# Seven instead of four SwiGLU pairs made of seven products, and where their weights' sums are made

## The chip, the cores and the metric

The kernel runs on one core of a Trainium2 chip. The time is that of one execution on the device, in microseconds, the median of several runs. The core has five engines that run beside each other and wait for one another by semaphores: PE (TensorE, matmuls into PSUM), DVE (VectorE) and ACT (ScalarE) for element-wise work, POOL (GpSimd), and SP (SyncE), which here issues all transfers between HBM and the core's SBUF from one queue, in a fixed order.

## The reference

A decoder block on 512 positions of 1024 channels, all in float32. Two token mixers run beside each other, are merged by gates, and are followed by a SwiGLU channel mixer with 2816 hidden channels:

```python
h = rmsnorm(x, norm1_g[l])
z = h @ w_in[l] + b_in[l]
z_glu, z_rx, z_rg, z_ga, z_gb = jnp.split(z, split_idx, axis=-1)
...                                   # y_a: convolution branch, y_b: recurrence branch
m = jax.nn.sigmoid(z_ga) * y_a + jax.nn.sigmoid(z_gb) * y_b
x = x + m @ w_mix_out[l]
h = rmsnorm(x, norm2_g[l])
x = x + (jax.nn.silu(h @ ffn_w1[l]) * (h @ ffn_w3[l])) @ ffn_w2[l]
```

and a last rmsnorm. The change concerns the last line quoted: the two products with ffn_w1 and ffn_w3, and the preparation of their weights and of those of ffn_w2.

## The kernel before, in words

**Numbers in two parts.** PE multiplies float32 values in a reduced form (F32R). Each operand is split into an upper part (a cast on ACT, L117) and a lower part (a subtraction on DVE or POOL, L113), and each product is made of three matmuls: upper by upper, upper by lower, lower by upper. Weights come in chunks of 128 x 1024 through four raw buffers (pool `raws`, RAW = 4) and are split into five `hl` buffers (HL = 5). `weights(key)` (L161) takes a chunk for use and first has the loads and splits of the next four chunks (AHEAD = 4) written into the program. Tiles named raw_x and hl_x in the profile belong to the chunk family x: in (w_in), lo and co (the mixers' output weights), mxb and mxt (w_mix_out), f (ffn_w1 and ffn_w3, plain), fb and ft (the same for seven products), ob and ot (ffn_w2).

**Stages.** The input stage multiplies by w_in (PE tiles z, g) in an order written out by hand (`ORDER`), with the convolution and the layer norm running beside it on DVE and ACT in small steps. The input stage's chunks have their lower parts made on POOL, all later ones on DVE. After it come the products of the recurrence branch (yb, 8 steps), of the convolution branch (ya, 8 steps), the mixing product (mxr), the SwiGLU stage (f, fr) and the output product (or).

**The SwiGLU stage.** The 22 tiles of 128 hidden channels go in 11 pairs (k, k + 11). A plain pair takes four chunks and 96 matmuls with 512 columns. Pairs in `SEVEN`, which are 2 to 5, use seven products of half-size blocks instead of eight (a Strassen-Winograd form, `ffn_seven`, L1011): seven chunks, called b11, b21, b22, t2, t1, t3, t4 in the order of use, and 168 matmuls with 256 columns, 24 a product. The b chunks are blocks of ffn_w1 and ffn_w3 side by side; the t chunks are sums of blocks.

**The weights' sums.** The t chunks are made earlier and kept in HBM. `make_f_sums` (L315) does so in the input stage, a piece at a time: from step 4 on, every third step of `ORDER`, it loads a piece (four quarters of 128 x 256, two transfers, tile fws, three buffers), makes four POOL operations from it two steps later, and stores it to `fs` (512 KB) five chunks later. There are four pieces a pair, 16 in all; whatever is left is done after the yb steps. The output weights ffn_w2 need the same kind of sums (`Quartered.make_sums`, L276): two raw buffers are loaded, DVE does four operations of 128 x 512 (tile ows), and four stores of 256 KB (ot) follow. These eleven are the last weights' sums. `out_sums(n)` (L959) writes n of them into the program: two after pair 1, one after each of pairs 3 and 5, two after each later pair until all are done.

**A pair's own work.** When both tiles of a pair exist, `Sevenfold.pair` (L825) makes from them what the output product needs: a split of 128 x 512 (ous), a sum and a split of 128 x 256 (os, os1p) and three subtractions of 128 x 256 (oe, ov). It stands at the end of the pair. The tiles live in a pool of 63 slots.

**Order.** Engines work through fixed queues. Outside the stretches written by hand, a planner that goes by estimated durations sets the order when the kernel is made; of what is ready it takes what comes earlier in the program. A buffer that comes free goes to the next tile in its pool. `issue_after` ties instructions behind a given one on its engine.

Of the kernel before, what the change touches and what calls it, by code (L numbers as in the profile page):

```python
# [8 lines left out]
F32 = mybir.dt.float32  # L9
F32R = mybir.dt.float32r  # L10
# [3 lines left out]
P = 128  # L14
T = 512
# [25 lines left out]

SEVEN = (2, 3, 4, 5)
SUMS_AT, SUMS_STEP, SUMS_LAG, STORE_LAG = 4, 3, 2, 5


ROWS = [
# [32 lines left out]
def tile_block(ctx, tc, a, out):  # L81
    nc = tc.nc
# [1 line left out]
    consts = pool("consts", 1)  # L84
    raws = pool("raws", RAW)
    hls = pool("hls", HL)
    wsums = pool("wsums", 3)
    psum = pool("psum", 6, space=bass.MemoryType.PSUM)
    psum2 = pool("psum2", 2, space=bass.MemoryType.PSUM)

# [131 lines left out]

    dram = ctx.enter_context(tc.tile_pool(name="dram", bufs=1, space=bass.MemoryType.DRAM))

    class Quartered:
        def __init__(self, name, w, kh, lo, parts=()):

            self.name, self.w, self.kh = name, w, kh
            self.parts = {n: [None] * kh for n in parts}
            self.sums = {(n, k): dram.tile([P, T], F32, tag=f"{name}{n}_{k}", name=f"{name}{n}_{k}") for n in ("t1", "t2", "t3", "t4") if n not in parts for k in range(kh)}  # L230
            self.at = {}

            def quarter(n, k):
                if n[0] == "t":
                    return self.sums[n, k][:, :]
# [40 lines left out]
        def make_sums(self, k):  # L276
            q = [raws.tile([P, 1024], F32, tag="raw", name=f"{self.name}ws{k}_{i}") for i in range(2)]
            for i, v in enumerate(q):
                nc.sync.dma_start(v, self.w[:, k + self.kh * i, :])
            (q11, q12), (q21, q22) = ((v[:, :T], v[:, T:]) for v in q)  # L280
            sub(vec, q22, q22, q12)
            sub(vec, q12, q12, q11)
            vec.tensor_tensor(out=q11, in0=q22, in1=q11, op=ALU.add)
            sub(vec, q21, q21, q11)
            for n, v in (("t1", q12), ("t2", q11), ("t3", q22), ("t4", q21)):
                if n in self.parts:
                    self.parts[n][k] = split(f"{self.name}{n}{k}", v, vec)
                else:
                    nc.sync.dma_start(self.sums[n, k][:, :], v)
# [4 lines left out]


    KF = NF // 2
    F_SUMS = ("t2", "t1", "t4", "t3")
# [7 lines left out]
    def f_chunk(n, k):  # L305
        def load(raw_t):
            if n[0] == "t":
                nc.sync.dma_start(raw_t, f_sums[k][:, F_SUMS.index(n), :])
            else:
                for i, w_ in enumerate((w1, w3)):  # L310
                    nc.sync.dma_start(raw_t[:, i * T : (i + 1) * T].rearrange("p (k n) -> p k n", k=4), f_quarter(n, k, w_, 0, 4))

        wchunk(f"f{n}_{k}", load, 8, P, lo=vec)

    def make_f_sums():  # L315

        todo = [(k, i, c) for k in SEVEN for i in range(2) for c in (0, 2)]
        sums_due, stores_due = [], []  # L320
        n = 0
        while todo or sums_due or stores_due:
            if stores_due and emitted[0] >= stores_due[0][0]:
                stores_due.pop(0)[1]()
            if sums_due and n >= sums_due[0][0]:
                sums_due.pop(0)[1]()
            if todo and n >= SUMS_AT and (n - SUMS_AT) % SUMS_STEP == 0:
                k, i, c = todo.pop(0)
                raw = wsums.tile([P, 1024], F32, tag="wsum", name=f"fws{k}_{i}_{c}")
                q = [raw[:, 256 * m : 256 * m + 256] for m in range(4)]  # L330
                four = (w1, w3)[i].rearrange("p (h k) (e n) -> p h k e n", h=2, e=2)
                with tc.issue_after(newest["load"]):
                    for h in range(2):
                        nc.sync.dma_start(
                            raw[:, h * T : h * T + T].rearrange("p (e k n) -> p e k n", e=2, k=2),
                            four[:, h, c : c + 2, :, k * P : (k + 1) * P].rearrange("p k e n -> p e k n"),
                        )

                def sums(raw=raw, q=q, k=k, at=T * i + P * c):
                    q11, q12, q21, q22 = q  # L340
                    with tc.issue_after(newest["sub"]):
                        sub(pool_e, q22, q22, q12)
                        sub(pool_e, q12, q12, q11)
                        pool_e.tensor_tensor(out=q11, in0=q22, in1=q11, op=ALU.add)
                        sub(pool_e, q21, q21, q11)

                    def stores():
                        with tc.issue_after(newest["load"]):
                            nc.sync.dma_start(f_sums[k][:, :, at : at + 256], raw.rearrange("p (m n) -> p m n", m=4))
# [443 lines left out]
            mixq.make_sums(j // 2 - 1)  # L793
    yb = sgb
    run_beside(1000)
    for _ in f_sums_steps:
        pass


    add = lambda o, x, y: vec.tensor_tensor(out=o, in0=x, in1=y, op=ALU.add)  # L800
# [8 lines left out]

    class Sevenfold:  # L810
        def __init__(self, q):
            self.q, self.uv, self.ops = q, [], []
            self.name, self.kh = q.name, q.kh

        def tile(self, j, make):

            k, i = j % self.kh, j // self.kh
            if i == 0:
                self.uv.append((longt(f"{self.name}u{k}"), longt(f"{self.name}v{k}")))
            for dst, cs in zip(self.uv[k], HALVES):  # L820
                make(cs, dst[:, HALVES[i]])
            if i:
                self.pair(k, *self.uv[k])

        def pair(self, k, ua, va):  # L825

            n = self.name
            u_ = split(f"{n}us{k}", ua, vec)
            s1 = shortt(f"{n}s1{k}")[:, LO]
            add(s1, va[:, LO], va[:, HI])  # L830
            sp = longt(f"{n}s1p{k}", F32R)
            split_to(sp[:, LO], sp[:, HI], s1, vec)
            e = longt(f"{n}e{k}")
            sub(vec, e[:, HI], ua[:, LO], va[:, LO])
            sub(vec, va[:, LO], s1, ua[:, LO])
            sub(vec, e[:, LO], ua[:, HI], va[:, LO])
            self.ops.append((u_, sp, e, va))
# [116 lines left out]


    o7 = Sevenfold(outq)
    sums_of = iter(range(KF))

    def out_sums(n):  # L959

# [50 lines left out]
    def ffn_seven(k):  # L1011
# [151 lines left out]
```

## Time and profile before

| | us |
|---|---|
| median of three runs | 814.86 (813.67 to 815.19) |
| the profiled execution | 814.89 |
| its span | 813.0 |
| PE busy | 800.0 |
| DVE busy | 644.1 |
| ACT busy | 443.1 |
| POOL busy | 210.3 |
| input stage, to the last z matmul | 325 |
| plain pairs 0 and 1 | 463 to 511 |
| pairs 2 to 5, seven products | 511 to 592 |
| plain pairs 6 to 10 | 592 to 700 |
| output product and end | 700 to 813 |

The span runs from the first to the last instruction that the profiler saw; the execution's own time is 1.9 us longer. In the profile's rows an instruction is named by engine, line, operation and out<-in; a line is often that of a helper (L113 the subtraction, L117 the cast, L441 three matmuls per product), so that tiles tell more than lines. In the timelines a row has its start, its length, the number of merged instructions, and in brackets how long the engine was idle before it and what ended that. The table of stretches gives for each stretch the busy time of every engine with the number of instructions, PE's granted clock as a share of full speed, the busy share of the DMA engines and their GB/s. Matmuls overlap, so that a matmul's listed duration is longer than its distance from the next.

### The profile page before, as it was taken

Reading aid. Unit: us, or ns where it says so; the run is one execution under the profiler, and the core shown is the slowest. Engines: PE = TensorE matmul, PEld = TensorE weight load, DVE = VectorE, ACT = ScalarE, POOL = GpSimd, SP = SyncE. Lnnn points to the kernel's source line nnn. Section 1 sums busy time; section 2 is a strip of 40 time slices with the busy share of each in tenths; the row PEclk is TensorE's granted clock in tenths of the full one; section 3 lists DMA queues with packets and bytes.
Section 4 is the critical chain, followed back from the end, with each engine's and each line's share of the span. In section 5 each row is a group of like instructions: output and inputs, shape, how many; then the busy total and the mean of one; then the engine's idle time right before and its main releaser. Section 6 shows DMA issues by size and latency. Waiting matters only on the chain.

```text
span 813.0 us, 11453 instructions
## 1 busy us (share of the span) xinstructions
PE 800.0 (98%) x4038; PEld 683.3 (84%) x4038; DVE 644.1 (79%) x1010; ACT 443.1 (55%) x626; POOL 210.3 (26%) x156
## 2 busy tenths in 40 slices
PE   8999999999999999999999999999999999999996
PEld 7988888888887888888888898999988888888884
DVE  4699899998999987777878769797875664688456
ACT  7546688776687755653336554364632223476442
POOL 3565768766675740000000042000000000000000
PEclk9999999999999999999999999999999999999998
DMA  6646475666654522358638535788778778576542
GB/s 209 193 123 171 136 202 176 189 193 198 186 170 130 182 75 65 116 171 263 217 104 259 156 97 176 238 262 248 224 247 282 249 271 297 177 250 216 169 160 104
DMA packets 182029, 153.46 MB, mean 189 GB/s; under 512 B 12519, under 2 KB 150163, under 8 KB 181971
## 3 DMA queue, kind: packets, MB, share of 16 engines
q1 hardware_dynamic: 181971, 152.72, 60.7%
q8 instruction: 32, 0.52, 0.3%
q14 instruction: 26, 0.21, 0.1%
HBM read 123.46 MB, written 26.21 MB: 184 GB/s over the span
## 4 chain that ended last, share of the span: by engine, by line
PE 93%; DVE 4%; issue 1%; DMA 1%; SPq 0%; POOL 0%; ACT 0%; POOLq 0%
PE z L441 31%; PE f L441 19%; PE or L844 13%; PE fr L1020 10%; PE yb L441 7%; PE ya L441 5%; PE mxr L844 5%; DVE cv L600 2%; PE g L721 2%; DMA raw_in<-in_w_in_dram 1%; PE th L481 0%; DVE xb L745 0%; PE tx L481 0%; DVE of L1086 0%; SPq L397 0%
## 5 line engine op out<-in xcount | busy, mean ns | idle before, releaser
L600 DVE SCALAR_TENSOR_TENSOR cv<-u,par,cv 128x511 f32<-128x511 f32 (+17 forms) x240 | 162.6, 729 | 1.1 <-ACT cv L597 0.9
L113 POOL TENSOR_TENSOR hl_in<-raw_in,hl_in 128x1024 fp32r<-128x1024 f32 x52 | 125.5, 2418 | 94.0 <-ACT hl_in L117 92.0
L117 ACT CAST hl_in<-raw_in 128x1024 fp32r<-128x1024 f32 x52 | 54.3, 1044 | 5.9 <-PE z L441 3.0
L117 ACT CAST hl_f<-raw_f 128x1024 fp32r<-128x1024 f32 x28 | 29.3, 1050 | 49.1 <-DMA raw_f<-in_ffn_w_dram 36.0
L113 DVE TENSOR_TENSOR hl_ob<-raw_ob,hl_ob 128x1024 fp32r<-128x1024 f32 (+1 forms) x23 | 27.1, 1178 | 26.8 <-ACT hl_ob L117 26.6
L113 DVE TENSOR_TENSOR hl_f<-raw_f,hl_f 128x1024 fp32r<-128x1024 f32 x28 | 36.2, 1304 | 14.3 <-ACT hl_f L117 14.2
L994 POOL TENSOR_TENSOR hf<-h20h,h20l 128x512 f32<-128x512 f32 x1 | 1.3, 1287 | 171.8 <-DVE h20l L485 171.8
L117 ACT CAST hl_ob<-raw_ob 128x1024 fp32r<-128x1024 f32 (+1 forms) x23 | 23.4, 1015 | 40.3 <-PE or L844 17.4
L441 PE MATMUL z<-h10h,hl_in 128*128 128x512 f32 (+1 forms) x112 | 42.4, 380 | 2.7 <-DVE h10l L485 1.5
L441 PE MATMUL z<-h15h,hl_in 128*128 128x512 f32 (+1 forms) x112 | 42.0, 376 | 0.0
L441 PE MATMUL z<-h16h,hl_in 128*128 128x512 f32 (+1 forms) x112 | 42.0, 376 | 0.0
L441 PE MATMUL z<-h17h,hl_in 128*128 128x512 f32 (+1 forms) x112 | 41.9, 376 | 0.0
L441 PE MATMUL z<-h11h,hl_in 128*128 128x512 f32 (+1 forms) x112 | 41.8, 375 | 0.0
L441 PE MATMUL z<-h12h,hl_in 128*128 128x512 f32 (+1 forms) x112 | 41.8, 375 | 0.0
L441 PE MATMUL z<-h14h,hl_in 128*128 128x512 f32 (+1 forms) x112 | 41.8, 375 | 0.0
L441 PE MATMUL z<-h13h,hl_in 128*128 128x512 f32 (+1 forms) x112 | 41.8, 375 | 0.0
L113 POOL TENSOR_TENSOR fws<-fws 128x256 f32<-128x256 f32 x48 | 36.3, 756 | 2.3
L113 DVE TENSOR_TENSOR ows<-ows,ows 128x512 f32<-128x512 f32 x22 | 15.2, 689 | 20.6 <-DMA ows<-in_ffn_w_dram 20.4
L113 DVE TENSOR_TENSOR hl_ot<-raw_ot,hl_ot 128x1024 fp32r<-128x1024 f32 (+1 forms) x17 | 20.1, 1191 | 11.1 <-ACT hl_ot L117 10.7
L441 PEld LDWEIGHTS z<-h10h,hl_in 128*128 128x128 f32 x112 | 21.3, 191 | 7.4 <-DVE h10l L485 1.8
L117 ACT CAST hl_ot<-raw_ot 128x1024 fp32r<-128x1024 f32 (+1 forms) x17 | 17.5, 1028 | 16.5 <-PE or L844 14.8
L441 PEld LDWEIGHTS z<-h15h,hl_in 128*128 128x128 f32 x112 | 21.4, 191 | 3.8
(905 smaller groups left out, 2574.9 us busy)
## 6 DMA issues: line engine op xcount, KB each, us to landing
raw_in<-in_w_in_dram SPq DMA_DIRECT2D x52, 512.0 KB
raw_f<-in_ffn_w_dram SPq DMA_DIRECT2D x28, 512.0 KB
ows<-in_ffn_w_dram SPq DMA_DIRECT2D x22, 512.0 KB
ot<-ows SPq DMA_DIRECT2D x44, 256.0 KB
raw_ob<-in_ffn_w_dram SPq DMA_DIRECT2D x33, 256.0 KB
raw_ot<-ot SPq DMA_DIRECT2D x33, 256.0 KB
fws<-in_ffn_w_dram SPq DMA_DIRECT2D x32, 256.0 KB
fs<-fws SPq DMA_DIRECT2D x16, 512.0 KB
```

The source lines that it names most:

```text
L113: return eng.tensor_tensor(out=o, in0=x, in1=y, op=ALU.subtract)
L117: copy(h, full)
L441: pe.matmul(ps, l, r, start=i == 0, stop=i == n - 1)
L600: vec.scalar_tensor_tensor(out=acc[c][:, s:], in0=u[c][:, : T - s], scalar=dw(c, s), in1=acc[c][:, s:], op0=ALU.mult, op1=ALU.add)
L721: pe.matmul(ps, l, r, start=k == 0, stop=k == len(mms) - 1)
L844: pe.matmul(banks[i], l_[:, ts], r_, start=start and n == 0, stop=stop and n == 2, skip_group_check=again)
L994: pool_e.tensor_tensor(out=v, in0=h2p[c][0].bitcast(F32), in1=h2p[c][1].bitcast(F32), op=ALU.add)
L1020: pe.matmul(ps[:, HALVES[i]], lw[:, 4 * i + c, :], rx_, start=not (again or i or c or m), stop=bool(i and c == 3 and m == 2), skip_group_c ...
```

## The change

- `SEVEN` grows to pairs 2 to 8. Three plain pairs become pairs of seven products.
- The input stage makes 28 pieces instead of 16. Steps 4 to 49 take every third step as before; from step 49 on (`SUMS_DENSE`) a piece starts at every second step, up to step 73. The generator goes on through the ya steps and is emptied after them. It could also make last weights' sums early (`OUT_EARLY`), which is set to none.
- The last weights' sums are placed by `OUT_SUMS`: four after pair 1, one after each of pairs 2 to 8, none later. The four results of one lie side by side in one HBM tile, and are stored in two transfers of 512 KB instead of four of 256 KB.
- A pair's own work is put in a waiting list. A pair of seven products no longer does it at its end: it is released in the middle of the next one, behind its second output block. Pairs 6, 7 and 8 keep it waiting (`keep = k - 6`), and plain pair 9 releases all three at its start. The tiles ous of pairs 0 to 2 go to the three buffers of the pieces, which have no other use by then.

```diff
-SEVEN = (2, 3, 4, 5)
+PIECES = 3
+OUT_EARLY = 0
+OUT_SUMS = {1: 4, 2: 1, 3: 1, 4: 1, 5: 1, 6: 1, 7: 1, 8: 1}
+SEVEN = (2, 3, 4, 5, 6, 7, 8)
 SUMS_AT, SUMS_STEP, SUMS_LAG, STORE_LAG = 4, 3, 2, 5
+SUMS_DENSE = 49
...
+            self.all_sums = [dram.tile([P, 4, T], F32, tag=f"{name}t_{k}", name=f"{name}t_{k}") for k in range(kh)]
...
+            if not self.parts:
+                for i, v in enumerate(q):
+                    nc.sync.dma_start(self.all_sums[k][:, 2 * i : 2 * i + 2, :], v.rearrange("p (m n) -> p m n", m=2))
+                return
...
-            if stores_due and emitted[0] >= stores_due[0][0]:
+            if stores_due and (emitted[0] >= stores_due[0][0] or not (todo or sums_due)):
...
-            if todo and n >= SUMS_AT and (n - SUMS_AT) % SUMS_STEP == 0:
-                k, i, c = todo.pop(0)
+            if todo and n >= next_at:
+                next_at += SUMS_STEP - (n >= SUMS_DENSE)
+                name, halves, dest = todo.pop(0)
...
-    for _ in f_sums_steps:
-        pass
...
-                self.pair(k, *self.uv[k])
+                self.waiting.append((k, *self.uv[k]))
+                self.release()
+
+        def release(self, keep=0):
+            while len(self.waiting) > keep:
+                self.pair(*self.waiting.pop(0))
...
-            u_ = split(f"{n}us{k}", ua, vec)
+            p_ = None
+            if n == "o" and k < PIECES:
+                both = wsums.tile([P, 1024], F32R, tag="wsum", name=f"{n}us{k}")
+                p_ = both[:, :T], both[:, T:]
+            u_ = split(f"{n}us{k}", ua, vec, p_)
...
         if n == 0:
             mixq.make_sums(3)
+        next(f_sums_steps, None)
+    for _ in f_sums_steps:
+        pass
...
         out_of(c12, u_[:, HI])
+        o7.release(max(0, k - 6))
         product(r7, "s3", "t3")
...
-        o7.pair(k, u_, v_)
+        o7.waiting.append((k, u_, v_))

     for k in range(1, KF):
         if k in SEVEN:
             ffn_seven(k)
-            out_sums(k % 2)
+            out_sums(OUT_SUMS.get(k, 0))
             continue
+        o7.release()
...
-        out_sums(2 if k < KF - 1 else KF)
+        out_sums(OUT_SUMS.get(k, 0))
```

More of the change, by code (lines that the diff above doesn't have):

```diff
@@ L86, in tile_block @@
     hls = pool("hls", HL)
-    wsums = pool("wsums", 3)
+    wsums = pool("wsums", PIECES)
     psum = pool("psum", 6, space=bass.MemoryType.PSUM)
@@ L223, in tile_block @@
     dram = ctx.enter_context(tc.tile_pool(name="dram", bufs=1, space=bass.MemoryType.DRAM))
+    IN_PLACE = ("t2", "t1", "t4", "t3")
     class Quartered:
@@ L229, in __init__ @@
             self.parts = {n: [None] * kh for n in parts}
-            self.sums = {(n, k): dram.tile([P, T], F32, tag=f"{name}{n}_{k}", name=f"{name}{n}_{k}") for n in ("t1", "t2", "t3", "t4") if n not in parts for k in range(kh)}
+            self.all_sums = [dram.tile([P, 4, T], F32, tag=f"{name}t_{k}", name=f"{name}t_{k}") for k in range(kh)]
+            self.sums = {(n, k): self.all_sums[k][:, i, :] for i, n in enumerate(IN_PLACE) if n not in parts for k in range(kh)}
             self.at = {}
@@ L234, in quarter @@
                 if n[0] == "t":
-                    return self.sums[n, k][:, :]
+                    return self.sums[n, k]
                 i, h = int(n[1]) - 1, int(n[2]) - 1
@@ L288, in make_sums @@
                 else:
-                    nc.sync.dma_start(self.sums[n, k][:, :], v)
+                    nc.sync.dma_start(self.sums[n, k], v)
     mixq = Quartered("mx", a["w_mix_out"][0].rearrange("(k p) n -> p k n", p=P), ND // 2, vec, ("t1", "t4"))
@@ L296, in tile_block @@
     KF = NF // 2
-    F_SUMS = ("t2", "t1", "t4", "t3")
     f_sums = {k: dram.tile([P, 4, 1024], F32, tag=f"fs{k}", name=f"fs{k}") for k in SEVEN}
@@ L307, in load @@
             if n[0] == "t":
-                nc.sync.dma_start(raw_t, f_sums[k][:, F_SUMS.index(n), :])
+                nc.sync.dma_start(raw_t, f_sums[k][:, IN_PLACE.index(n), :])
             else:
@@ L315, in make_f_sums, with f_piece, o_piece @@
     def make_f_sums():
-        todo = [(k, i, c) for k in SEVEN for i in range(2) for c in (0, 2)]
+        def f_piece(k, i, c):
+            four = (w1, w3)[i].rearrange("p (h k) (e n) -> p h k e n", h=2, e=2)
+            at = T * i + P * c
+            halves = [four[:, h, c : c + 2, :, k * P : (k + 1) * P].rearrange("p k e n -> p e k n") for h in range(2)]
+            return f"{k}_{i}_{c}", halves, f_sums[k][:, :, at : at + 256]
+        def o_piece(k, c):
+            four = outq.w.rearrange("p (h k) (e n) -> p h k e n", h=2, e=2)
+            cs = slice(256 * c, 256 * c + 256)
+            return f"o{k}_{c}", [four[:, h, k, :, cs] for h in range(2)], outq.all_sums[k][:, :, cs]
+        todo = [f_piece(k, i, c) for k in SEVEN for i in range(2) for c in (0, 2)]
+        todo += [o_piece(k, c) for k in range(OUT_EARLY) for c in range(2)]
         sums_due, stores_due = [], []
-        n = 0
+        n, next_at = 0, SUMS_AT
         while todo or sums_due or stores_due:
-            if stores_due and emitted[0] >= stores_due[0][0]:
+            if stores_due and (emitted[0] >= stores_due[0][0] or not (todo or sums_due)):
                 stores_due.pop(0)[1]()
@@ L326, in make_f_sums, with sums @@
                 sums_due.pop(0)[1]()
-            if todo and n >= SUMS_AT and (n - SUMS_AT) % SUMS_STEP == 0:
-                k, i, c = todo.pop(0)
-                raw = wsums.tile([P, 1024], F32, tag="wsum", name=f"fws{k}_{i}_{c}")
+            if todo and n >= next_at:
+                next_at += SUMS_STEP - (n >= SUMS_DENSE)
+                name, halves, dest = todo.pop(0)
+                raw = wsums.tile([P, 1024], F32, tag="wsum", name=f"fws{name}")
                 q = [raw[:, 256 * m : 256 * m + 256] for m in range(4)]
-                four = (w1, w3)[i].rearrange("p (h k) (e n) -> p h k e n", h=2, e=2)
                 with tc.issue_after(newest["load"]):
[L333 to L339, printed above, removed]
+                    for h, src in enumerate(halves):
+                        to = raw[:, h * T : h * T + T]
+                        to = to.rearrange("p (e k n) -> p e k n", e=2, k=2) if len(src.shape) == 4 else to.rearrange("p (e n) -> p e n", e=2)
+                        nc.sync.dma_start(to, src)
+                def sums(raw=raw, q=q, dest=dest):
                     q11, q12, q21, q22 = q
@@ L348, in stores @@
                         with tc.issue_after(newest["load"]):
-                            nc.sync.dma_start(f_sums[k][:, :, at : at + 256], raw.rearrange("p (m n) -> p m n", m=4))
+                            nc.sync.dma_start(dest, raw.rearrange("p (m n) -> p m n", m=4))
                     stores_due.append((emitted[0] + STORE_LAG, stores))
@@ L811, in __init__ @@
         def __init__(self, q):
-            self.q, self.uv, self.ops = q, [], []
+            self.q, self.uv, self.ops, self.waiting = q, [], [], []
             self.name, self.kh = q.name, q.kh
@@ L956, in tile_block @@
     o7 = Sevenfold(outq)
-    sums_of = iter(range(KF))
+    sums_of = iter(range(OUT_EARLY, KF))
     def out_sums(n):
@@ L1065, in tile_block @@
             ffn_out(j, p1, p3)
-        out_sums(2 if k < KF - 1 else KF)
+        out_sums(OUT_SUMS.get(k, 0))
+    assert next(sums_of, None) is None
     x2 = [[longt(f"x2b{t}{h}") for h in range(2)] for t in range(NT)]
```

## The prediction

> **What bounds the kernel now.** I read the page's busy times first, then the chain that ended last, the table of stretches over the SwiGLU stage, and there the timelines of SP's queue and of DVE. The page and the chain say that PE is the bound and that the pairs stand on the path back to back:
>
> ```profile
> span 813.0 us, 11453 instructions
> ...
> PE 800.0 (98%) x4038; PEld 683.3 (84%) x4038; DVE 644.1 (79%) x1010; ACT 443.1 (55%) x626; POOL 210.3 (26%) x156
> ...
> 480.34 30.60 PE f L441 x169
> 510.94 80.63 PE fr L1020 x672
> 591.57 108.83 PE f L441 x480
> ```
>
> PE is idle for 13 us of 813.0, and nowhere between 480.34 and 700.40. The four pairs made of seven products (fr, 672 matmuls, 168 a pair) take 80.63 us: 20.16 a pair, 120.0 ns a matmul, 2.88 us a product of 24. The five plain pairs (f, 480 matmuls, 96 a pair) take 21.77 each, 226.7 ns a matmul. Next, what the other engines do in these stretches (pair 1 plain, pairs 2 to 5 of seven products, pair 8 plain with two last weights' sums):
>
> ```profile
> core 0: us, PE busy (x) PEld busy (x) DVE busy (x) ACT busy (x) POOL busy (x), PEclk, DMA share, GB/s
> 480.40:511.00 30.60, 30.60 (x171) 26.77 (x170) 29.45 (x46) 15.49 (x22) 11.97 (x7) 1.00 0.53 171
> 511.00:531.00 20.00, 20.00 (x169) 20.00 (x168) 15.37 (x26) 8.97 (x13) 0.00 (x0) 1.00 0.80 245
> 531.00:551.30 20.30, 20.30 (x171) 20.30 (x171) 17.81 (x27) 13.01 (x20) 0.00 (x0) 1.00 0.82 249
> 551.30:571.40 20.10, 20.10 (x170) 20.10 (x169) 15.67 (x24) 9.98 (x15) 0.00 (x0) 1.00 0.83 253
> 571.40:591.60 20.20, 20.20 (x170) 20.20 (x169) 17.09 (x27) 12.05 (x18) 0.00 (x0) 1.00 0.73 220
> ...
> 635.10:656.90 21.80, 21.80 (x98) 18.06 (x97) 12.73 (x22) 6.12 (x8) 0.00 (x0) 1.00 0.84 272
> ```
>
> The reader is to see that pair 1's stretch has DVE full (29.45 of 30.60), and that a pair of seven products already has DVE at 15 to 18 of 20 and the DMA engines at 0.8. PE's fullness there is not slack: it depends on weights that come just in time. The place where they come latest is the head of pair 2. SP's queue and DVE there:
>
> ```profile
> 489.81 0.34 SPq L308 DMA_DIRECT2D raw_ft<-fs  x1
> 493.48 5.12 SPq L279 DMA_DIRECT2D ows<-in_ffn_w_dram  x2
> ...
> 503.61 0.33 SPq L279 DMA_DIRECT2D ows<-in_ffn_w_dram  x1
> ...
> 508.48 0.33 SPq L279 DMA_DIRECT2D ows<-in_ffn_w_dram  x1
> 509.10 1.31 SPq L308 DMA_DIRECT2D raw_ft<-fs  x2
> 513.34 6.04 SPq L289 DMA_DIRECT2D ot<-ows  x4
> 520.39 0.32 SPq L308 DMA_DIRECT2D raw_ft<-fs  x1
> 520.82 0.38 SPq L311 DMA_DIRECT2D raw_fb<-in_ffn_w_dram  x1
> ...
> 507.86 1.22 DVE L113 TENSOR_TENSOR hl_ft<-raw_ft,hl_ft 128x1024 fp32r<-128x1024 f32 x1
> ...
> 512.62 0.69 DVE L113 TENSOR_TENSOR ows<-ows,ows 128x512 f32<-128x512 f32 x1 [0.56 <-DMA ows<-in_ffn_w_dram]
> ...
> 518.35 0.68 DVE L113 TENSOR_TENSOR ows<-ows,ows 128x512 f32<-128x512 f32 x1
> ...
> 519.29 2.35 DVE L113 TENSOR_TENSOR hl_ft<-raw_ft,hl_ft 128x1024 fp32r<-128x1024 f32 x2
> ...
> 525.93 1.23 DVE L113 TENSOR_TENSOR hl_ft<-raw_ft,hl_ft 128x1024 fp32r<-128x1024 f32 x1 [2.78 <-ACT hl_ft L117]
> ```
>
> The four raw buffers go round in the order of the program: t2 of pair 2 (489.81), the two halves of the first last weights' sum (493.48 and, at the row's end, 498.28), the two of the second (503.61, 508.48), and only then t1 and t3 of pair 2 (509.10, 510.10) and t4 (520.39). The 509.10 load starts as t2's split ends (507.86 + 1.22 = 509.08); t4's load and the next one (520.82) start once the second sum's stores (the last at 519.06) have landed. PE reaches the products t1, t3, t4 of pair 2 at 510.94 plus 4, 5 and 6 times 2.88: 522.46, 525.34, 528.22. Their splits end at about 520.5, 521.6 and 527.16. So with two sums ahead of them t1 and t4 are ready 2.0 and 1.1 us before PE wants them.
>
> **The change, part by part.**
>
> **1. Three more pairs (6, 7, 8) of seven products.** PE: 3 x (21.77 - 20.16) = 4.8 us saved, all on the path. The Trainium skill's page "TensorE: Matmul & The Clock Gate", section "Back-to-back issue gap", gives N/2.4 + 2.5 ns, as an estimate 109 ns for 256 columns and 216 for 512, so 18.3 and 20.7 us a pair, 7.1 us for three, and 816.7 us in all with the other steps below. The 672 and 480 matmuls above show 120.0 and 226.7, the measurement decides, and that larger gain gets no chance.
>
> **2. Four last weights' sums after pair 1 instead of two (L1066, L276).** The two added ones (call them third and fourth) take their four buffers before t1, t3, t4 of pair 2. A sum holds its buffers about 12 us from its second load: 498.28 to 510.10 is 11.8, 508.48 to 520.82 is 12.3. The third sum's second load goes out where t3's did, at 510.10, so t1 can load at about 522.1. From load to the end of the split t4 took 520.39 to 527.16 = 6.8 us: t1 is ready at 528.9. PE wants its lower half at the third matmul, 522.46 + 0.24: a wait of 6.2 us. t3 follows by a split (1.2) and is in time. t4 loads into the buffer that t1 gives back, 528.9 + 6.8 = 535.7, while PE wants it at 528.22 + 6.2 + 0.24 = 534.7: 1.1 more. Together 7.3 us of PE idle. Lower end: if DVE does the third sum's four operations (0.69 each) as soon as its load is there (4.1 us after 510.10, as 508.48 to 512.62) and its store lands in 1.8 (519.06 to 520.82), t1 loads at 518.8 and is ready at 525.6: 2.9 for t1, and the same 1.0 for t4: 3.9. Upper end: t4 has to wait for the fourth sum's buffers, 520.82 + 12.0 + 6.8 = 539.6: 11.1. I take 7.3, because DVE is full up to 519.29 with pair 1's own work, which comes earlier in the program.
>
> **3. One sum after each of pairs 2 to 8.** How far a split is ahead of PE is a lead; without a sum it grows, a sum eats it. Rows of pairs 3 to 5:
>
> ```profile
> 540.75 1.22 DVE L113 TENSOR_TENSOR hl_ft<-raw_ft,hl_ft 128x1024 fp32r<-128x1024 f32 x1
> ...
> 546.86 1.22 DVE L113 TENSOR_TENSOR hl_fb<-raw_fb,hl_fb 128x1024 fp32r<-128x1024 f32 x1
> ...
> 553.58 0.68 DVE L113 TENSOR_TENSOR ous3l<-ou,ous3h 128x512 fp32r<-128x512 f32 x1
> ...
> 556.65 0.42 DVE L113 TENSOR_TENSOR os1p<-os,os1p 128x256 fp32r<-128x256 f32 x1
> ...
> 563.89 1.23 DVE L113 TENSOR_TENSOR hl_ft<-raw_ft,hl_ft 128x1024 fp32r<-128x1024 f32 x1 [2.03 <-ACT hl_ft L117]
> ...
> 570.77 1.23 DVE L113 TENSOR_TENSOR hl_fb<-raw_fb,hl_fb 128x1024 fp32r<-128x1024 f32 x1 [0.68 <-ACT hl_fb L117]
> ```
>
> Product n of these 28 starts at 510.94 + 2.88 n. t4 of pair 2 (n = 6) has 1.1 us of lead, t3 of pair 3 (n = 13, split done 541.97) has 6.4: 0.76 gained per product. b22 of pair 4 (n = 16, 548.08) has 8.9, and t4 of pair 4 (n = 20, 565.12), past one sum, 3.4: a sum costs 5.5 us. After a wait at t4 the lead is 0, three products later 2.3; 2.3 - 5.5 would be a wait of 3.2 a pair. But o7.release moves the pair's own work (the 553.58 row and five operations of 0.42 like the 556.65 row, 2.8 us) out of the sum's way, to behind c12, so the wait is 0.4 for pairs 3 to 6, and I take none for 7 and 8, which have no pair's work at all: 1.6 us. Ends: 0, and 6 x 3.2 = 19.2 if the move helps nothing. DVE then has some 17.8 of 20.16 a pair (65.9 in the four stretches, less two sums of 2.8, over four, plus one sum), and the DMA engines 3.67 + 2.1 MB in 20.16 us = 286 GB/s where the rows show 220 to 272. Merging the stores (44 to 22) and the first pairs' splits in freed wsums buffers move no bytes and cost nothing in the sum.
>
> **4. Pairs 6 to 8 released at pair 9.** Three times 2.8 us on DVE at once. Cover: a plain pair with two sums has DVE at 12.73 of 21.80; two sums less (5.5) and three pairs more give 15.6. Nothing.
>
> **5. Twelve more pieces at the input stage's end.** 48 POOL operations, 24 loads and 12 stores on SP, some 12 MB, from about 265 us on. Rows that bear on it:
>
> ```profile
> L113 POOL TENSOR_TENSOR fws<-fws 128x256 f32<-128x256 f32 x48 | 36.3, 756 | 2.3
> ...
> 260.00:314.00 54.00, 54.00 (x239) 44.69 (x239) 46.44 (x66) 34.22 (x42) 27.80 (x16) 1.00 0.40 119
> 314.00:332.00 18.00, 18.00 (x81) 14.90 (x80) 13.00 (x21) 10.14 (x18) 0.00 (x0) 1.00 0.22 66
> 332.00:380.00 48.00, 48.00 (x213) 39.74 (x212) 38.36 (x53) 26.39 (x38) 0.00 (x0) 1.00 0.58 185
> ...
> 301.39 6.40 DVE L623 TENSOR_TENSOR lnmt<-lnmt,u 128x512 f32<-128x512 f32 x6
> ...
> 308.47 0.69 DVE L113 TENSOR_TENSOR lnmsl<-lnmt,lnmsh 128x512 fp32r<-128x512 f32 x1 [0.69 <-ACT lnmsh L117]
> ...
> 313.70 0.46 PE lnmp L611 x2
> ...
> 481.29 4.01 DVE L113 TENSOR_TENSOR hl_f<-raw_f,hl_f 128x1024 fp32r<-128x1024 f32 x2
> ```
>
> POOL has 27.80 us in 54 and then nothing, the DMA engines 0.22 to 0.58: room for 36 us and 12 MB. What is late next is PE's mean over channels (lnmp, 313.70), 4.5 us behind its input (309.16). DVE slows beside POOL: the two splits at 481.29 took 2.0 us each, against 1.22 where POOL rests. Seven 512-wide DVE operations ahead of lnmp (the 301.39 and 308.47 rows), each held by at most one POOL operation of 0.756, lose 5.3: a wait of 0.8 at most, nothing likelier, since POOL is not always there. The Trainium skill's page "SBUF — State Buffer", section "Who interferes with whom", names the reason, an exclusive lock that a DVE instruction with two SBUF inputs and a GpSimd instruction that reads SBUF take in turn; the 481.29 row agrees, and by that rule the same 0.8 is the end.
>
> **The sum.** -4.8 + 7.3 + 1.6 = +4.1 us. The profiled execution took 814.89 us, with 813.0 of span and 1.9 around it, 0.03 from the median 814.86: predicted 819.0.
>
> **The rivals.**
> B, faster: the third and fourth sums cost nothing, because the queue's fixed order puts t1, t3 and t4 of pair 2 ahead of them, or the sums find their time in pair 1. Price 0 for step 2, and a lead of several us then carries step 3: 814.89 - 4.8 = 810.1. It decides at t1's split ending by 522.7. For it: SP's order is fixed when the kernel is made, and PE never waited here. Against it: each buffer above went to the next load in program order.
> C, much slower: DVE and four buffers don't keep up with a sum beside every pair, 3.2 us each as above: 814.89 - 4.8 + 7.3 + 19.2 = 836.6. For it: from b22's split of pair 4 to that of pair 5 (546.86 and 570.77 above, 1.2 later each) 23.9 us went by, and PE took 20.16. Against: that stretch began with 8.9 us of lead, and the pair's work stood in it.
> D, no change: step 2 at its lower end, 3.9, step 3 at 0 to 1.6: 814.0 to 815.6.
>
> **How the numbers follow.** Forecast (step 2 at 6 to 11, step 3 at 0 to 4: 816.5 to 825.0) 0.57; D 0.13; B 0.22; C 0.08. The range 810.0 to 825.0 leaves out C and a little of each end; the forecast's own is 816.5 to 825.0. Faster 0.22, same 0.13, slower 0.65, by 0.2% (1.6 us), about what this kernel's measurement can tell.
>
> **What would show it.** Right: fr in the chain at about 141 us for 1176 matmuls plus waits of PE for hl_ft in pair 2 near 522 to 535; in SP's queue eight ows loads before raw_ft of t1; later pairs each with a short wait at t4. Step 1 is wrong if a matmul of fr isn't 120 ns. Step 2 is wrong if raw_ft goes before the fifth ows load; step 3 if the leads of pairs 3 to 8 grow, or PE waits over 1 us in each; step 5 if PE waits at lnmp or for hl_lo.

## The result and the profile after

The changed kernel takes 836.82 us (median of 5 runs, 834.73 to 838.36); the kernel before, run beside it, 813.67 (813.39 to 815.19). The ratio is 1.0276, with a 95% interval of 1.0251 to 1.03: it is slower by 23 us. Predicted were 819.0, with a range of 810.0 to 825.0. The profiled execution took 838.08 us, 23.2 above that of before (814.89).

The page of the changed kernel, its span and its line of busy times:

```profile
span 836.3 us, 12036 instructions
...
PE 804.2 (96%) x4254; PEld 693.3 (83%) x4254; DVE 669.6 (80%) x1034; ACT 459.3 (55%) x650; POOL 255.5 (31%) x204
```

PE is busy for 4.2 us more and idle for 32 instead of 13. A table of stretches, one for each pair of seven products (2 to 8, from the first matmul of one to the first of the next), says where. Its columns are the stretch, its length, the busy time of PE, its weight loads, DVE, ACT and POOL, the granted clock, the DMA share and GB/s:

```profile
510.89:546.45 35.56, 23.73 (x169) 22.82 (x168) 21.61 (x36) 10.48 (x17) 0.00 (x0) 0.81 0.81 259
546.45:566.69 20.24, 20.24 (x170) 20.21 (x169) 14.00 (x20) 8.69 (x12) 0.00 (x0) 1.00 0.83 262
566.69:589.01 22.32, 20.81 (x170) 20.20 (x168) 16.86 (x27) 10.63 (x16) 0.00 (x0) 1.00 0.87 263
589.01:611.13 22.12, 21.02 (x168) 20.41 (x169) 17.84 (x26) 11.47 (x17) 0.00 (x0) 1.00 0.87 259
611.13:633.19 22.06, 21.09 (x170) 20.27 (x168) 17.09 (x27) 10.72 (x16) 0.00 (x0) 1.00 0.77 247
633.19:657.94 24.75, 21.68 (x168) 20.46 (x169) 17.01 (x26) 10.57 (x16) 0.00 (x0) 1.00 0.76 241
657.94:680.57 22.63, 21.87 (x168) 21.67 (x169) 16.04 (x20) 11.12 (x15) 0.00 (x0) 0.92 0.93 279
```

| stretch | before, us | after, us | difference |
|---|---|---|---|
| pair 2 | 20.16 | 35.56 | +15.4 |
| pairs 3 to 5 | 60.48 (3 x 20.16) | 64.68 | +4.2 |
| pairs 6 to 8 | 65.31 (3 x 21.77) | 69.44 | +4.1 |
| output product and finish | 112.76 | 112.18 | -0.6 |

Together +23.1, which is the whole difference but for 0.1. Pairs 9 and 10, plain in both, take 21.79 and 21.76. Two thirds of the loss lie in one pair. SP's queue, then DVE, then PE there:

```profile
517.57 2.12 SPq L298 DMA_DIRECT2D ot<-ows  x2
521.45 0.33 SPq L290 DMA_DIRECT2D ows<-in_ffn_w_dram  x1
521.88 0.86 SPq L298 DMA_DIRECT2D ot<-ows  x2
522.79 1.37 SPq L290 DMA_DIRECT2D ows<-in_ffn_w_dram  x1
527.58 1.41 SPq L322 DMA_DIRECT2D raw_ft<-fs  x2
532.12 1.05 SPq L298 DMA_DIRECT2D ot<-ows  x2
534.23 0.32 SPq L322 DMA_DIRECT2D raw_ft<-fs  x1
```

```profile
521.59 0.69 DVE L120 TENSOR_TENSOR ows<-ows,ows 128x512 f32<-128x512 f32 x1
529.95 0.69 DVE L120 TENSOR_TENSOR ows<-ows,ows 128x512 f32<-128x512 f32 x1 [7.67 <-DMA ows<-in_ffn_w_dram]
...
532.98 1.23 DVE L120 TENSOR_TENSOR hl_ft<-raw_ft,hl_ft 128x1024 fp32r<-128x1024 f32 x1 [0.15 <-ACT hl_ft L124]
534.72 1.23 DVE L120 TENSOR_TENSOR hl_ft<-raw_ft,hl_ft 128x1024 fp32r<-128x1024 f32 x1 [0.52 <-ACT hl_ft L124]
```

```profile
522.28 0.28 PE L1060 MATMUL fr<-hs_0h,hl_ft 128*128 128x256 f32 x1
533.00 0.58 PE L1060 MATMUL fr<-hs_0h,hl_ft 128*128 128x256 f32 x1 [10.43 <-ACT hl_ft L124]
...
539.11 0.41 PE L1060 MATMUL fr<-hs_1h,hl_ft 128*128 128x256 f32 x1
```

The third sum's last DVE operation ends at 522.28. Its two stores go out at 521.88 and 522.36, the fourth sum's two loads at 521.45 and 522.79. Only at 527.58 and 528.66 can t1 and t3 of pair 2 be loaded into the buffers which these stores give back. DVE itself stands still for 7.67 us, for the fourth sum's load, so it is not what is short. PE, which wanted t1 at 522.4, gets it at 533.0, and then runs t1's product until 539.11: 6.1 us instead of 2.88. The table of stretches, cut at these points, shows why:

```profile
522.40:533.00 10.60, 0.17 (x3) 0.01 (x1) 2.79 (x5) 1.63 (x2) 0.00 (x0) 0.66 0.89 300
533.00:536.00 3.00, 2.54 (x10) 2.24 (x11) 2.43 (x2) 1.05 (x1) 0.00 (x0) 0.50 1.02 362
536.00:539.10 3.10, 3.10 (x16) 3.10 (x16) 0.00 (x0) 0.00 (x0) 0.00 (x0) 0.50 0.83 148
539.10:542.40 3.30, 3.18 (x26) 2.98 (x24) 1.38 (x2) 1.04 (x2) 0.00 (x0) 0.95 1.01 283
```

The granted clock of PE is 0.50 for the 6 us after the wait and 0.95 in the next 3.3. In the waits of PE (operation waited for, us in total, times, longest) between 500 and 690 us, the first row is pair 2's, and the others are mostly the small waits of pairs 4 to 8, the longest of them 1.4 us, for the first chunk of pair 8:

```profile
PE fr L1060 <- ACT hl_ft L124: 10.6, 2, 10.4
PE fr L1060 <- DVE hl_fb L120: 3.0, 5, 0.8
PE fr L1060 <- DVE hl_ft L120: 2.9, 7, 0.8
PE fr L1060 <- ACT hl_fb L124: 2.2, 3, 1.4
```

Behind ACT stands the DMA. In the waits of ACT from 546 to 681 us the two largest are for landings, that is for loads which had gone out late:

```profile
ACT hl_ft L124 <- DMA raw_ft<-fs: 38.8, 21, 4.8
ACT hl_fb L124 <- DMA raw_fb<-in_ffn_w_dram: 17.4, 9, 4.0
```

The low clock of pair 8 (0.92 in its stretch) is one stretch at half clock. It follows the wait of 1.4 us, which ends at 657.94, and another of 0.8, which ends at 659.20:

```profile
658.90:662.20 3.30, 3.00 (x14) 3.00 (x15) 3.13 (x5) 2.94 (x5) 0.00 (x0) 0.50 0.93 307
```

### The profile page after: what moved, and what is told of

Its sections match the earlier page's. It is cut to its first block, busy times and chain, and to the rows that moved or that the text cites. A ratio compares the mean times of both kernels' runs of the same rounds, so it can differ in the third digit from the quotient of the medians.

```text
span 836.3 us, 12036 instructions
## 1 busy us (share of the span) xinstructions
PE 804.2 (96%) x4254; PEld 693.3 (83%) x4254; DVE 669.6 (80%) x1034; ACT 459.3 (55%) x650; POOL 255.5 (31%) x204
## 4 chain that ended last, share of the span: by engine, by line
PE 70%; DMA 12%; DVE 11%; issue 2%; ACT 2%; SPq 2%; POOL 1%; ACTq 0%; POOLq 0%; DVEq 0%
PE z L468 29%; PE or L880 12%; PE f L468 8%; PE yb L468 7%; PE ya L468 5%; PE mxr L880 5%; DMA raw_fb<-in_ffn_w_dram 5%; DMA raw_ft<-fs 3%; PE fr L1060 3%; DVE cv L627 2%; PE g L748 2%; DVE hl_fb L120 2%; DMA ot<-ows 2%; DVE hl_ft L120 1%; DMA raw_in<-in_w_in_dram 1%
## 5 line engine op out<-in xcount | busy, mean ns | idle before, releaser
L120 POOL TENSOR_TENSOR fws<-fws 128x256 f32<-128x256 f32 x84 | 70.2, 838 | 67.5 <-DMA fws<-in_ffn_w_dram 63.7
L124 ACT CAST hl_ft<-raw_ft 128x1024 fp32r<-128x1024 f32 x28 | 29.4, 1050 | 54.9 <-DMA raw_ft<-fs 54.8
L1060 PE MATMUL fr<-hs_0h,hl_ft 128*128 128x256 f32 x224 | 44.3, 294 | 11.1 <-ACT hl_ft L124 10.4
L120 DVE TENSOR_TENSOR hl_ft<-raw_ft,hl_ft 128x1024 fp32r<-128x1024 f32 x28 | 34.2, 1222 | 24.1 <-ACT hl_ft L124 24.1
L1060 PEld LDWEIGHTS fr<-hs_0h,hl_ft 128*128 128x128 f32 x224 | 37.3, 201 | 11.8 <-ACT hl_ft L124 10.6
L120 DVE TENSOR_TENSOR hl_fb<-raw_fb,hl_fb 128x1024 fp32r<-128x1024 f32 x21 | 26.7, 1275 | 9.6 <-ACT hl_fb L124 9.4
L124 ACT CAST hl_fb<-raw_fb 128x1024 fp32r<-128x1024 f32 x21 | 22.1, 1051 | 22.3 <-DMA raw_fb<-in_ffn_w_dram 17.7
L1060 PE MATMUL fr<-hs_0l,hl_ft 128*128 128x256 f32 x112 | 32.7, 292 | 0.0
L120 DVE TENSOR_TENSOR hl_ot<-raw_ot,hl_ot 128x1024 fp32r<-128x1024 f32 (+1 forms) x17 | 20.1, 1191 | 11.1 <-ACT hl_ot L124 10.7
```

Source lines behind the costliest of these rows:

```text
L120: return eng.tensor_tensor(out=o, in0=x, in1=y, op=ALU.subtract)
L124: copy(h, full)
L1060: pe.matmul(ps[:, HALVES[i]], lw[:, 4 * i + c, :], rx_, start=not (again or i or c or m), stop=bool(i and c == 3 and m == 2), skip_group_c ...
```

## The experiments

The theory after this reading: raw buffers, not DVE and not the DMA engines' rate, are short; a sum that holds two of the four keeps the pair's own loads back. The rivals: DVE has too much to do beside a pair; the DMA engines can't move a pair's weights and a sum's together; merging the stores, or moving the earlier pairs' work, does the harm. "Beside" in what follows means beside a pair of seven products. The time of a pair runs from its first matmul to the next pair's.

**Two sums after pair 1, as before.** The last two of the eleven go behind pair 9.

```diff
-OUT_SUMS = {1: 4, 2: 1, 3: 1, 4: 1, 5: 1, 6: 1, 7: 1, 8: 1}
+OUT_SUMS = {1: 2, 2: 1, 3: 1, 4: 1, 5: 1, 6: 1, 7: 1, 8: 1, 9: 2}
```

> The changed kernel with two last weights' sums after pair 1 instead of four, and the other two after pair 9. In the changed kernel pair 2 took 35.6 us (20.16 without waits) and pairs 3 to 8 took 134.1 (121.0 without waits). Theory A (the two added sums stand in the buffers ahead of t1, t3, t4): pair 2 goes back to 20 to 21 us, pairs 3 to 8 stay at about 22 each, total 836.8 - 15 = 822. Rival (the longer stores or the sums beside the pairs make pair 2's wait too): pair 2 stays above 27 us, total 829 or more.

Measured: 825.21 us, 1.0138 of before (1.012 to 1.0155). Pair 2 is back at 20.23, so its 15.4 us hang on the third and fourth sum. The pairs after it take 20.16, 23.2, 24.28, 21.89, 25.52 and 20.15: a sum beside each still costs 14.2 us over six times 20.16, no less than in the changed kernel (13.1). That part is a cost of its own, and not the aftermath of pair 2. In each of pairs 4 to 7 the longest wait of PE is not for a chunk but for ACT's copy of a product (c or q): 2.1, 1.6, 0.8 and 1.7 us. Before the first of them, ACT stood still for a late load, with that copy behind it in its fixed queue:

```profile
561.07 1.04 ACT L124 CAST hl_ft<-raw_ft 128x1024 fp32r<-128x1024 f32 x1 [2.79 <-DMA raw_ft<-fs]
562.02 0.58 ACT L1072 COPY c<-fr 128x512 f32<-128x512 f32 x1
```

So a late load can stop PE before its own chunk is due.

**The stores as before.** A sum is stored in four transfers instead of two.

```diff
-                for i, v in enumerate(q):
-                    nc.sync.dma_start(self.all_sums[k][:, 2 * i : 2 * i + 2, :], v.rearrange("p (m n) -> p m n", m=2))
+                for n, v in (("t1", q12), ("t2", q11), ("t3", q22), ("t4", q21)):
+                    nc.sync.dma_start(self.sums[n, k], v)
```

> The changed kernel with each sum's four results stored as they are made, 256 KB each, into the same tile, instead of two stores of 512 KB. Theory B (a buffer comes back some 3 us later because its one store is twice as long and starts last): pair 2's excess of 15.4 us falls to about 9, each later pair from 22.1 to about 21.2, total near 825. Rival (the stores' form moves nothing, as my prediction had it): 836 to 837.

Measured: 840.52, 1.0322 (1.0293 to 1.0352), not faster than the changed kernel. Pair 2 takes 34.54, the next six 20.15, 21.98, 21.73, 25.25, 21.5 and 24.91. The merged stores cost at most 1.0 us, in pair 2.

**No sum beside pairs 3 to 8.** Their seven sums move behind pairs 9 and 10; the four after pair 1 stay.

```diff
-OUT_SUMS = {1: 4, 2: 1, 3: 1, 4: 1, 5: 1, 6: 1, 7: 1, 8: 1}
+OUT_SUMS = {1: 4, 9: 4, 10: 3}
```

> The changed kernel with no sum beside pairs 3 to 8: four after pair 1 as in the change, four after pair 9, three after pair 10. Theory C (a sum beside each pair costs each pair 2 us): pairs 3 to 8 take 20.2 us each, 121 instead of 134; pair 2 stays at 35; pairs 9, 10 and the output product's start pay for seven sums. Rival (the pairs' own seven chunks are too much for the queue without any sum): pairs 3 to 8 stay at 22. The total says little, 825 to 845.

Measured: 850.70, 1.0446 (1.0425 to 1.0468), above the 825 to 845 that were expected. Pair 2 takes 34.41, and each of pairs 3 to 8 takes 20.16: with no sum beside it a pair has no wait, and the six of them, pairs 3 to 8, run without a gap. The sums beside them therefore cost the changed kernel 134.1 - 121.0 = 13.1 us. They pay for themselves all the same: here the output product and the finish take 140.41 instead of 112.18, and among the waits of PE stands

```profile
PE or L880 <- ACT hl_ob L124: 20.2, 3, 12.6
```

a wait in the output product, which eats sums as fast as PE goes and finds them late.

**The pair's own work back at its end.** On top of the first experiment, the elementwise work of an earlier pair, which the change had moved behind c12, goes back to a pair's end.

```diff
-        o7.release(max(0, k - 6))
         product(r7, "s3", "t3")
...
         o7.waiting.append((k, u_, v_))
+        o7.release(max(0, k - 5))
```

> e1_two_first with a pair's own work at its end again instead of in the middle of the next pair (pairs 6 to 8 still wait). e1 had pairs 4 to 7 at 23.2, 24.3, 21.9, 25.5 us. My step 3: the move takes 2.8 us a pair out of the sum's way, so without it pairs 3 to 6 take 2 to 3 us more each, total 825.2 + 8 = 833. Rival: DVE isn't what a sum is short of, the buffers are, and the total stays within 3 us of 825.2.

Measured: 822.63, 1.0096 (1.0082 to 1.011), 2.6 us less than the first experiment. The pairs take 20.27, 22.16, 26.91, 21.39, 20.44, 20.16 and 20.16. The move, for which the prediction had given 2.8 us a pair as a gain, gains nothing.

**Four sums after pair 1 in the kernel before**, and nothing else of the change.

```diff
-        out_sums(2 if k < KF - 1 else KF)
+        out_sums(4 if k == 1 else 2 if k < KF - 1 else KF)
```

> The kernel before with four last weights' sums after pair 1 instead of two, and nothing else (the later ones then end two sums sooner). Theory A: the two added sums alone make the wait at t1 of pair 2, 15 us, pair 3 takes 20.2, total 813.9 + 15 = 829. Rival (they need the changed kernel's other parts to do harm): under 820.

Measured: 826.83, 1.0152 (1.0139 to 1.0165). Pair 2 takes 32.73, pairs 3 to 5 take 20.15 to 20.16. The two added sums alone bring most of the loss of pair 2. In SP's queue the fourth sum's first load goes out at 520.44, and t1's load at 525.87. They bring the wait and the slow clock too; the wait of PE, and the table of stretches around it:

```profile
PE fr L1020 <- ACT hl_ft L117: 9.3, 1, 9.3
```

```profile
522.20:531.00 8.80, 0.06 (x1) 0.00 (x0) 2.91 (x5) 1.12 (x2) 0.00 (x0) 0.78 0.96 335
531.00:534.00 3.00, 1.98 (x7) 1.69 (x8) 2.45 (x2) 1.55 (x2) 0.00 (x0) 0.50 0.88 309
```

**Three sums after pair 1 in the kernel before.**

```diff
-        out_sums(2 if k < KF - 1 else KF)
+        out_sums(3 if k == 1 else 2 if k < KF - 1 else KF)
```

> The kernel before with three sums after pair 1. Four gave pair 2 32.7 us, 12.6 over. My step 2 counted 7.3 for the third sum's own hold of the buffers, as if nothing ran beside it. Theory F (the rest is the fourth sum: its two loads of 512 KB go out between the third sum's stores and slow them, and PE's granted clock is halved for some 6 us after so long a wait): pair 2 takes 26 to 28.5 us, total 820 to 822. Rival (the third sum alone does it, and the fourth costs nothing): 31 to 33 us, total 825 to 827.

Measured: 821.78, 1.0082 (1.0064 to 1.01). Pair 2 takes 27.49, 7.3 more than without the third sum, and pair 3 takes 21.39. In SP's queue t1 now loads at 519.93, before the third sum's last stores have gone out: it takes a buffer of the second sum, the place that the fourth sum's first load had in the run with four. Below are that queue, the waits of PE, and two stretches, the second all at half clock:

```profile
519.93 0.38 SPq L308 DMA_DIRECT2D raw_ft<-fs  x1
520.45 2.46 SPq L289 DMA_DIRECT2D ot<-ows  x3
522.96 3.44 SPq L308 DMA_DIRECT2D raw_ft<-fs  x2
```

```profile
PE fr L1020 <- ACT hl_ft L117: 3.8, 1, 3.8
PE fr L1020 <- DVE hl_ft L113: 0.5, 1, 0.5
```

```profile
522.30:529.00 6.70, 2.82 (x11) 2.52 (x12) 1.49 (x2) 1.53 (x3) 0.00 (x0) 0.72 0.91 297
529.00:532.00 3.00, 3.00 (x16) 3.00 (x15) 1.23 (x1) 1.89 (x2) 0.00 (x0) 0.50 1.06 316
```

The 7.3 us are 4.3 of waiting, and the other 3.0 go mostly on the half clock. That this equals the 7.3 of the prediction's step 2 is luck: that sum was for four sums, with t1 in a buffer of the third. The fourth sum is worth 32.73 - 27.49 = 5.2 us more: it takes the second sum's buffers, and t1 has to wait for the third's, from 519.93 to 525.87.

**The sums in buffers of their own.** A last weights' sum takes its tiles from the pool wsums, which is idle by then, instead of the raw buffers; the first pairs' splits, which the change had put into wsums, return to where they were. Pair 8 is plain again, and o7 keeps one pair more; these come with the edit, and their shares were not measured apart.

```diff
-SEVEN = (2, 3, 4, 5, 6, 7, 8)
+SEVEN = (2, 3, 4, 5, 6, 7)
...
-            q = [raws.tile([P, 1024], F32, tag="raw", name=f"{self.name}ws{k}_{i}") for i in range(2)]
+            pool_, tag_ = (raws, "raw") if self.parts else (wsums, "wsum")
+            q = [pool_.tile([P, 1024], F32, tag=tag_, name=f"{self.name}ws{k}_{i}") for i in range(2)]
...
-            if n == "o" and k < PIECES:
+            if False:
...
-        o7.release(max(0, k - 6))
+        o7.release(max(0, k - 5))
```

> The last weights' sums in the three wsums buffers instead of two of the four raw ones; the first pairs' splits go back to the 63 slots, for which pair 8 becomes plain again (pairs 2 to 7 of seven products). Four sums after pair 1, one after each of 2 to 8. Theory S (what is short is raw buffers): pair 2 and pairs 3 to 7 take 20.2 us each, total 813.7 - 2 x 1.6 = 810.5. Theory W (what is short is the transfers' rate, 5.8 MB a pair against some 290 GB/s): pair 2 much better than 35, pairs 3 to 7 still at 21 to 22, total 815 to 822.

Measured: 817.42, 1.004 (1.003 to 1.005). Pair 2 takes 26.89, and pairs 3 to 7 take 20.16 each, with a sum beside every one of them. That is the verdict on pairs 3 to 8: the buffers were short. Pair 2 now waits for something else:

```profile
PE fr L1061 <- ACT c L1073: 1.9, 1, 1.9
PE fr L1061 <- DVE hs_1l L120: 1.4, 1, 1.4
PE fr L1061 <- ACT hs_1h L124: 1.2, 1, 1.2
```

The four early sums, no longer held back by buffers, reach DVE sooner and push back the sums of pair 2's input (hs), which DVE makes in pair 1. These waits are 4.5 of pair 2's 6.7 us; behind them the granted clock is 0.50 for 3.3 us (524.8 to 528.1).

**The same without sums after pair 1.**

```diff
-OUT_SUMS = {1: 4, 2: 1, 3: 1, 4: 1, 5: 1, 6: 1, 7: 1, 8: 1}
+OUT_SUMS = {2: 1, 3: 1, 4: 1, 5: 1, 6: 1, 7: 1, 8: 2, 9: 2, 10: 1}
```

> As e4_own_buffers, with no sum after pair 1, one after each of pairs 2 to 7, two after 8 and 9, one after 10. In e4 pairs 3 to 7 took 20.16 us, and pair 2 took 26.9 because two early sums pushed DVE's sums of the pairs' inputs back. Theory S (only raw buffers were short, and DVE in pair 1): pair 2 goes to 20.2 too, total 813.9 - 2 x 1.6 = 810.7, faster than before. Rival (pair 2 still waits, or the sums after 8 to 10 hold up the output product): 813 to 818.

Measured: 811.74, 0.9969 (0.9958 to 0.998). Pair 2 takes 21.51, pairs 3 to 7 take 20.16.

**The same with pair 8 of seven products again**; only pair 0's split lies in wsums. The lines stand against the changed kernel; the sums' buffers and `o7.release(max(0, k - 5))` are as in the two runs above.

```diff
-OUT_SUMS = {1: 4, 2: 1, 3: 1, 4: 1, 5: 1, 6: 1, 7: 1, 8: 1}
+OUT_SUMS = {2: 1, 3: 1, 4: 1, 5: 1, 6: 1, 7: 1, 8: 1, 9: 2, 10: 2}
 SEVEN = (2, 3, 4, 5, 6, 7, 8)
...
-            if n == "o" and k < PIECES:
+            if n == "o" and k == 0:
```

> As e5 with pair 8 of seven products again: two wsums buffers for the sums, the third for the first pair's split, two sums after 9 and 10, one after each of 2 to 8. Theory S: all seven pairs at 20.2 us, total 813.9 - 3 x 1.6 = 809.1. Rival (two buffers are too few for a sum a pair, or sums after pair 10 come too late): some pairs at 21 to 23 us or a longer output product, total 812 to 820.

Measured: 809.31 (808.82 to 813.97 in eight runs), 0.9951 (0.9933 to 0.9968): faster than the kernel before by 4.8 us, and than the changed one by 27.5. All seven pairs take 20.15 to 20.16. Its page, its chain of work, and three of its pairs (2, 5 and 6) in the table of stretches:

```profile
span 807.5 us, 12048 instructions
...
PE 795.6 (99%) x4254; PEld 689.4 (85%) x4254; DVE 667.9 (83%) x1034; ACT 457.6 (57%) x650; POOL 253.6 (31%) x204
```

```profile
510.87 141.11 PE fr L1061 x1176
```

```profile
510.70:530.87 20.17, 20.17 (x170) 20.16 (x169) 19.80 (x34) 11.72 (x17) 0.00 (x0) 1.00 0.78 254
571.20:591.30 20.10, 20.10 (x170) 20.10 (x169) 19.39 (x32) 12.26 (x18) 0.00 (x0) 1.00 1.03 326
591.30:611.50 20.20, 20.20 (x171) 20.20 (x169) 16.30 (x22) 10.37 (x14) 0.00 (x0) 1.00 0.96 322
```

The chain runs through 1176 matmuls in one piece, 120.0 ns each. DVE is busy for 19.80 and 19.39 us of a pair, more than in any pair of seven products of the changed kernel but the 35.56 us one, the DMA engines move 326 GB/s against the changed kernel's 241 to 279, and PE waits for neither. Both rivals, DVE and the DMA rate, fall with these two rows.

**The twelve added pieces alone**, in the kernel before; their sums are made and stored, and nothing uses them.

```diff
-        todo = [(k, i, c) for k in SEVEN for i in range(2) for c in (0, 2)]
+        todo = [(k, i, c) for k in (*SEVEN, 6, 7, 8) for i in range(2) for c in (0, 2)]
...
-            if todo and n >= SUMS_AT and (n - SUMS_AT) % SUMS_STEP == 0:
+            if todo and n >= next_at:
+                next_at += SUMS_STEP - (n >= 49)
...
-    for _ in f_sums_steps:
-        pass
...
+        next(f_sums_steps, None)
+    for _ in f_sums_steps:
+        pass
```

> The kernel before with the twelve more pieces at the input stage's end, and nothing else (the sums for pairs 6 to 8 are made and stored, and not used). My step 5: the recurrence branch's products start where they do before (324.9 us) within 0.5, total 813.9 to 814.7. Rival (POOL's 48 more operations hold DVE or the loads up): 816 or more.

Measured: 813.65 beside 814.59, 0.9989 (0.9979 to 0.9998). The pieces cost nothing.

## Why the prediction was right or wrong

The direction was right. The time was not: 836.82 against 819.0 and outside the range. The prediction's sum was -4.8 + 7.3 + 1.6 = +4.1. As the runs have it, the terms are -4.8 + 15.4 + 13.1, and the end 0.6 shorter: +23.1.

**Step 1, -4.8: right.** A pair of seven products that waits for nothing takes 20.16 us, a plain one 21.77, with seven of them as with four, and in the best version the whole 4.8 reaches the time. The estimate from the Trainium skill's page "TensorE: Matmul & The Clock Gate" (section "Back-to-back issue gap"), whose formula the section gives for an isolated matmul, is 109 ns. It is not borne out here: 1176 of them took 141.11 us, 120.0 each.

**Step 2, +7.3 with ends 3.9 and 11.1: the order of the buffers right, the size wrong, 15.4.** As said, eight loads of last weights stand in SP's queue before t1 of pair 2, and PE waits for hl_ft from 522.4 on. The term for t4 came out as well: it loads at 534.23, when t1's split has ended (532.98 + 1.23), and PE waits 0.8 us for it against 1.1. Two terms failed.
- The time at which t1 can load. The prediction took the third sum's stores to go out by 520.3 and to land in 1.8 us, so that t1 loads at 522.1. In fact they went out at 521.88 and 522.36, and gave the buffers back at 527.58 and 528.66, 5.7 and 6.3 us later. The 1.8 was misread: the load at 520.82 went out before the store of 519.06 had landed (521.06 by the trace's record of landings, 2.0 us), and the store that freed t4's buffer took 2.9 (517.45 to 520.32). Those were quarters of 256 KB. Around the third sum's stores the fourth sum's two loads go out (521.45 and 522.79), and the first, second and fourth sum's stores of 512 KB landed in 2.6 to 4.1 us. That the overlap with loads is what slows the landing fits this and the DMA share of 0.89 there; it was not tried by itself, and it is not special to these loads, since later sums' stores took up to 6.6 us.
- What a wait costs. The prediction counted a wait as its own length. After it PE ran at half clock, and t1's product took 6.1 us instead of 2.88. Of the 15.4, PE's waits are 11.8 (10.6 and 1.2 in the waits of pair 2), the slow product is another 2.8 (3.2 less the 0.47 of a wait inside it), and most of the other 0.8 is hidden in the listed durations: a matmul is listed with 0.28 us where the next could start 0.12 after it, so that its end runs into a wait. The Trainium skill's page "TensorE: Matmul & The Clock Gate", section "Part 1: The HAM clock gate", says that after an idle window of about 3.4 us PE falls to half its clock and comes back after about as long a busy one. The rows agree that it falls: after 3.8 us of waiting with three sums and after 10.4 here, the granted clock is 0.50. They show it coming back after about 6 us. But shorter waits brought it too, as 1.4 and 0.8 close together did ahead of pair 8.

In the changed kernel pair 2 is 2.8 us longer than with four sums in the kernel before. At most 1.0 of it is the merged stores; the rest stays open.

**Step 3, +1.6 with ends 0 and 19.2: wrong, 13.1.** The failed term is the credit for moving the pair's own work: "so the wait is 0.4 for pairs 3 to 6". The bookkeeping of leads (0.76 gained a product, 5.5 lost to a sum) gave 3.2 a pair without that credit, and 2.2 were measured on average, from 0.1 in pair 3 to 4.6 in pair 7. With the work back at the pair's end the kernel was 2.6 us faster, not slower. The credit counted DVE's time, and DVE was not what was late: t3, t4 and b11 wait for loads, which wait for raw buffers. The sign that the prediction gave for a failure of step 3, waits of PE over 1 us in each pair, came in the main: PE is idle for 0.8 to 3.1 us in the stretches of pairs 4 to 8, in pieces of at most 0.8 us but for the one of 1.4, and not at all in pair 3. Of the 13.1, this idle time is 7.4 (134.1 less 126.7 busy). The half clock in pair 8 gives that stretch 1.7 us more busy time than 20.16. The other 4.0 is again listed durations that run into waits: counted by the distances between the starts of matmuls, less 0.12 each, pairs 3 to 8 lose 10.4 us in breaks of over 0.3, 1.2 at half clock outside these, and 1.6 in shorter breaks.

**Steps 4 and 5 and the merged stores, nothing: right.** Pairs 9 and 10 take 21.79 and 21.76 with the three released pairs' work in pair 9; the added pieces alone gave 0.9989 of before; the stores taken apart again gave no better time. PE's mean in the input stage, on which a wait of 0.8 at most was feared, showed none.

**The rivals.** C came out at 836.6, 0.2 us from what was measured, and was given 0.08. That the totals agree is luck: it had 7.3 in pair 2 and 19.2 in the others, and the runs show 15.4 and 13.1. But its reason, that four buffers don't keep up with a sum beside every pair, was half right (the buffers, not DVE), and the evidence given for it, 23.9 us from one split of b22 to the next where PE took 20.16, was better than the one against it. B's time, 810.1, is close to what the best version takes (809.31), by way of buffers of their own and with no sum after pair 1: then the sums do find their time.

## What to carry to other kernels

To price work that is slipped in beside a full pipeline, follow who gets its buffers next, and not only which engine has time left. Sums that went through the pipeline's own four buffers cost 15.4 us where four stood ahead of one pair and 13.1 where one stood beside each of six. In buffers of their own the single ones cost nothing; the four at once still cost 6.7, because they went ahead of the next pair's input on DVE, and had to be spread out. A wait of PE is to be priced with the half clock that may follow it: some 3 us here after waits of 3.8 and 10.4 us, 1.7 after two short ones close together. A store that must land before a buffer is free is not to be priced at its best time: stores of one size landed in 2.6 to 6.6 us in one kernel.

## What the runs showed of the hardware

- After a wait of 3.8 us, and of 10.4 us, PE's granted clock stood at 0.50. After the longer one it did so for about 6 us, in which a product of 24 matmuls took 6.1 us instead of 2.88. After the waits of at most 0.8 us in pairs 4 and 5 the granted clock stayed at 1.00. The length of one wait does not decide it in between: waits of 1.4 and 0.8 us close together ahead of pair 8 were followed by 3.3 us at 0.50 (658.9 to 662.2), while after the wait of 2.1 us in pair 4 of the first experiment the clock stayed at 1.00 (562.5 to 566.0).
- The 16 DMA engines moved 322 to 326 GB/s through two pairs on end (571.2 to 611.5) beside a PE that never waited, where the kernel before had 220 to 272.
- By the traces' record of landings, a 512 KB store of last weights landed 2.6 to 6.6 us after it went out in the changed kernel (22 of them), and a 256 KB store 2.0 to 3.8 us after it in the kernel before (44).
